# Two table-sized edits: which engine copies the inverses' PSUM products, and behind what one weight of the second feed-forward is cast

## The chip, the cores and the metric

The kernel runs on one core of a Trainium2 chip. Its time is device microseconds of one execution. The core's engines have an instruction queue each and meet only at semaphores: TensorE (PE; PEld is its weight load), VectorE (DVE), ScalarE (ACT), GpSimd (POOL), and SyncE (SP), which issues nearly all DMAs. Before the change the median of three runs was 1485.09 us (1483.22 to 1487.64).

## What is computed

One layer of a diffusion backbone: 512 latent tokens and 256 context tokens of width 1024, all in float32.

```
x   = post_ln(ALPHA*x + 0.5*gate*swiglu(modulate(x)))          # half-step feed-forward 1 (and for ctx)
p   = modulate(x) @ w_in                                        # q,k,v of both mixers, gates
o_a = neighbourhood attention over (latent grid + context)
o_b = gated delta rule, forward and backward, chunks of 64 tokens
y   = (sigmoid(ga)*(o_a @ w_pa) + sigmoid(gb)*(o_b @ w_pb)) @ w_o
x   = post_ln(ALPHA*x + gate*y)
x   = post_ln(ALPHA*x + 0.5*gate*swiglu(modulate(x)))          # half-step feed-forward 2
```

The delta rule needs, for each chunk, head and direction, the inverse of a unit lower triangular matrix:

```
m  = where(strict, (beta*k) @ k.T * decay, 0)
uw = triangular_solve(eye + m, rhs, unit_diagonal=True)
```

## The kernel before, in words

**Products.** Every large product is made in three passes: an operand is split into a rounded high part (cast on ACT, line 137, tiles `wh`, `uxh`) and the rest (subtraction on DVE, line 139, tiles `wl`, `uxl`), and PE multiplies high by high, high by low and low by high (lines 193 to 195).

**Order of the work.** The program is written as one stream of instructions; a scheduler that plays it through on a modelled timeline then sets the order on each engine. `tc.issue_after(x)` holds what stands under it back until x has been placed. So an edit of one line can reorder all engines for some distance behind it. Once set, an engine's order is fixed: an instruction that waits holds up everything behind it on its engine.

**The delta rule's stage** runs from about 785 to 957 us. The work goes over three blocks (`bi` = 0, 1, 2) of two steps (`st` = 0, 1); each step has two pairs of heads, both directions together. `grams` builds the matrices m (tiles `Bt`) and writes them to DRAM; `base_inverse` inverts their 32x32 diagonal blocks on DVE, row by row (lines 1165 and 1166, tiles `bt` and `Xt`; its matrix `L` comes from DRAM, line 1158, and its diagonal is set on POOL, line 1161), and writes the result to DRAM (line 1169). `inverse(bi, st)`, called six times, loads these blocks as `T0` and `T1` (line 1186), transposes them on DVE (1188, 1189), and joins them to 64x64 and then 128x128 inverses. It does so in a chain between PE and the engines that can read PSUM:

- PE: `py` = Bt x T0 (32x32 tiles); copy to `Y` (line 1208); PE: `p0`, `p1` from `Y`; `p0` back into `T6` (DVE, 1224), `p1` into `Tt` (ACT, 1225);
- PE: `py` = Bt x T6 (64x64 tiles); copy to `Y6` (line 1235); PE: `p1` from `Y6` and `Tt`; `p1` into `Tt` (ACT, 1243).

There is one `T6` (`NT6` = 1): the copies of `T0` into it (ACT, 1199) for the next inverse wait until PE has read it for this one. `scan_step` then uses `Tt`: `r` (DVE, 1266), a PE product with `Tt`, `vn` (DVE, 1275), `ktail` (ACT, 1280), products with both, the state `S` (DVE, 1290). Between these short products PE works off the projections' tiles (`pm`, lines 193 to 195), put there by `turn`, so that a chain's waits are covered as far as the order allows. ACT also casts these projections' weights and spills their results.

**The second feed-forward** begins at about 1121 us. The last product before it, with `w_o`, ends token block by token block: for blocks t = 0 to 3 `finish2` adds the residual, normalises twice, and makes `y` (ACT, line 130; its bias `nb` is made on DVE, line 129), which PE transposes (line 148) into `uxh`, `uxl`. The first four hidden tiles are computed on the first half of the tokens while blocks 2 and 3 are still being normalised. The weights' casts for these tiles are held by a table, `ws.behind`: for weight j a pair, behind which ACT's cast and DVE's subtraction may be placed. The eighth weight (j = 7) was held on ACT behind `y` of block 2.

Of the kernel before, what the change touches and what calls it, by code (L numbers as in the profile page):

```python
# [58 lines left out]
def body(ctx, tc, I, out, dbg=None):  # L59
    nc = tc.nc  # L60
    V, S, G, T = nc.vector, nc.scalar, nc.gpsimd, nc.tensor
# [15 lines left out]
    def tl(p, shape, tag, bufs=1, dt=F32):  # L77
        uid[0] += 1
        return p.tile(list(shape), dt, name=f"{tag}_{uid[0]}", tag=tag, bufs=bufs)
# [265 lines left out]
    def rows(w, ks):  # L345
        return [w[k * P:(k + 1) * P, :] for k in ks]
# [23 lines left out]
    def order1():  # L370
        t = lambda fs: [I["up1"][2 * f + j] for f in fs for j in range(2)]
        dn = lambda a, b: rows(I["dn1"], range(a, b))
        o = t(range(F0, N1)) + t(range(N1)) + dn(0, N1) + dn(0, N1 - 2)
        return [(w, "x") if j % 3 == 1 else w for j, w in enumerate(o)]
# [60 lines left out]
    ws = Stream(wp, order1(), WB, 1)  # L435
# [242 lines left out]
    ws = Stream(wp, o, WB, 1)  # L678
# [90 lines left out]
    ws = ws2  # L769
# [284 lines left out]
    def mm(*a, **k):  # L1054
        last[0] = T.matmul(*a, **k).ins  # L1055
# [14 lines left out]
    def turn(kind, i):  # L1070

        due[0] += RATE[kind][i]
        while due[0] >= 1:
            due[0] -= 1
            with tc.issue_after(last[0]):
                next(fills, None)
# [102 lines left out]
    def inverse(bi, st, rd, Bts):  # L1179


        T0 = tl(gq, [P, 8, 32], "T0", 2)
        T1 = tl(gq, [P, 8, 32], "T1", 2)
        for dst, d in ((T1, 0), (T0, 1)):
            for q in range(2):
                nc.sync.dma_start(dst[q:P:2, 4 * d:4 * d + 4], bass.AP(rd.tensor, rd.offset + (2 * d + q) * 16384 + st * 2048, [[32, 64], [2 * 2048, 4], [1, 32]]))
        fl = lambda t, m: t[:, m:m + 4].rearrange("p m c -> p (m c)")
        V.transpose(fl(T0, 0), fl(T1, 0))
        V.transpose(fl(T1, 4), fl(T0, 4))
        blk = [slice(32 * b, 32 * b + 32) for b in range(4)]  # L1190


        T6, Tt = T6s[inv_n[0] % NT6], Tts[inv_n[0] % NTT]
        inv_n[0] += 1
        sysm = lambda b: slice(0, 4) if b % 2 else slice(4, 8)
        bt = lambda k, b: Bts[k % 2][:, k // 2 + (0 if b else 2)]
        for b, r in enumerate(blk):
            o = 32 * (b % 2)
            S.copy(T6[r, :, o:o + 32], T0[r])
            G.tensor_copy(Tt[r, :, 32 * b:32 * b + 32], T1[r])  # L1200
        py = tl(pgq, [P, 4, 32], "pi", 2)
        for k in range(4):
            for b, r in enumerate(blk):
                q, m = blk[b ^ 1], k if b % 2 else 4 + k
                mm(py[r, k, :], bt(k, b % 2)[q, r], T0[q, m, :], start=True, stop=True, tile_position=(32 * (b ^ 1), 32 * b))
        turn("i", bi)
        Y = tl(gq, [P, 4, 32], "Y2", 2)
        V.tensor_copy(Y[:], py[:])
        p0 = tl(pgq, [P, 4, 32], "pi", 2)
        p1 = tl(pgq, [P, 4, 32], "pi", 2)  # L1210
        for k in range(4):
            for b, r in enumerate(blk):
                m = k if b % 2 else 4 + k
                mm(p0[r, k, :], T1[r, m, :], Y[r, k, :], start=True, stop=True, tile_position=(32 * b, 32 * b))
        turn("i", bi)
        for k in range(4):
            for b, r in enumerate(blk):
                m = k if b % 2 else 4 + k
                mm(p1[blk[b ^ 1], k, :], Y[r, k, :], T1[r, m, :], start=True, stop=True, tile_position=(32 * b, 32 * (b ^ 1)))
        turn("i", bi)  # L1220
        for b, r in enumerate(blk):
            o = 32 * ((b + 1) % 2)
            q = blk[b ^ 1]
            V.tensor_scalar(T6[r, sysm(b), o:o + 32], p0[r], -1.0, None, op0=ALU.mult)
            S.activation(Tt[q, sysm(b), r], p1[q], AF.Copy, scale=-1.0)

        hb = [slice(0, 64), slice(64, 128)]
        py = tl(pgq, [P, 4, 64], "pi", 2)
        for k in range(4):
            for b in range(2):  # L1230
                m = k if b else 4 + k
                mm(py[hb[b], k, :], bt(k, b)[hb[1 - b], hb[b]], T6[hb[1 - b], m, :], start=True, stop=True, tile_position=(64 * (1 - b), 64 * b))
        turn("i", bi)
        Y6 = tl(gq, [P, 4, 64], "Y6")
        V.tensor_copy(Y6[:], py[:])
        p1 = tl(pgq, [P, 4, 64], "pi", 2)
        for k in range(4):
            for b in range(2):
                m = k if b else 4 + k
                mm(p1[hb[1 - b], k, :], Y6[hb[b], k, :], Tt[hb[b], m, hb[b]], start=True, stop=True, tile_position=(64 * b, 64 * (1 - b)))  # L1240
        turn("i", bi)
        for b in range(2):
            S.activation(Tt[hb[1 - b], sysm(b), hb[b]], p1[hb[1 - b]], AF.Copy, scale=-1.0)
        return [[Tt[:, 4 * d + 2 * i + p] for d in range(2) for i in range(2)] for p in range(2)]
# [99 lines left out]
    def inv_of(bi, st):  # L1344
        inv[(bi, 2 * st)], inv[(bi, 2 * st + 1)] = inverse(bi, st, rds[bi], [res[(bi, 2 * st + p)][0] for p in range(2)])
# [278 lines left out]
    ys, norms = [], []  # L1624
# [26 lines left out]
    ws = Stream(wp, [(w, key(j)) if key(j) else w for j, w in enumerate(src)], WB, 2)  # L1651
    ws.extra = {"b": (wb, 4, wp, WB), "c": (wc, 2, wp, WB)}

    ws.behind = {j: (norms[t]["y"], norms[u][m]) for j, t, u, m in ((2, 1, 2, "nb"), (3, 1, 2, "nb"), (4, 2, 3, "x2"), (5, 2, 3, "x2"), (6, 2, 3, "nb"), (7, 2, 3, "nb"))}

    def h2(p, n):
        hs.append((tl(p, [P, NX], "hh", n, F32R), tl(p, [P, NX], "hl", n, F32R)))
# [128 lines left out]
    ws = Stream(wp, [(w, "d") if j % 6 > 1 else w for j, w in enumerate(rows(I["dn2"], range(NF)))], WB, 2)  # L1786
# [23 lines left out]
    for t in range(4):  # L1810
        h = tl(lp, [P, D], "h4", 2)
        n, m = (512, D) if t < 3 else (D // PIECES, 512)
        st = tl(lp, [P, PIECES, 6], "bst", 4)
        x2 = tl(lp, [P, D], "x2", 2)
# [123 lines left out]
```

## Time and profile before

| | before |
|---|---|
| median of the runs | 1485.09 us |
| profiled execution, its own time | 1482.26 us |
| its span, first to last instruction | 1480.5 us |
| mean granted TensorE clock | 0.995 |
| PE busy | 1430.8 us (97%) |
| DVE busy | 1144.0 us (77%) |
| ACT busy | 661.7 us (45%) |
| DMA queue of SP | 229.40 MB, 45.8% of 16 engines' span |

A matmul's end is modelled, so PE's share says that it is seldom without an instruction, not that it runs at its peak. The timeline view lists an engine's instructions with start, length and, in brackets, how long the engine stood idle before one and what released it. `T<-rd` means: into tile T from rd. The profile drops the numbers of tiles; the order listings below keep them, so that two tiles of one name can be told apart there.

### The profile page before, as it was taken

To read this page: it belongs to the slowest core of one execution; us is meant where nothing else is said; L and a number is where in the kernel's file an instruction comes from. 1 tells how busy PE (TensorE), PEld (TensorE's weight loads), DVE (VectorE), ACT (ScalarE), POOL (GpSimd) and SP (SyncE) were. 2 spreads that over 40 slices of the span, in tenths; PEclk is the share of its full clock that TensorE was granted. 3 is DMA by queue.
4 is the path that set the end of the run, shared out by engine and by line. 5 is a ranking of instruction groups with operands and counts; after the bars stand their busy time and mean duration, and the time that the engine had idled before them with its cause. 6 is when DMAs were issued, how large, how long until landed. Compare 5 with 4: busy or idle time off the path is not lost.

```text
span 1480.5 us, 23912 instructions
## 1 busy us (share of the span) xinstructions
PE 1430.8 (97%) x9117; PEld 1255.9 (85%) x9117; DVE 1144.0 (77%) x1975; ACT 661.7 (45%) x1090; POOL 214.6 (14%) x262
## 2 busy tenths in 40 slices
PE   6999999999999999999999899999999999999997
PEld 4789889999997777888877778877788999998886
DVE  8688869999987666768787885676668799886627
ACT  5435523434333387545544434376426454444310
POOL 1000000000000111223201001352321022220001
PEclk9999999999999999999999999999999999999999
DMA  9677764444569444222476523283344133234722
GB/s 377 206 250 250 240 232 172 162 161 165 164 212 400 181 160 150 79 93 94 153 227 209 163 68 126 93 302 108 120 157 171 38 129 114 94 106 144 257 99 85
DMA packets 109236, 248.56 MB, mean 168 GB/s; under 512 B 29049, under 2 KB 44481, under 8 KB 109121
## 3 DMA queue, kind: packets, MB, share of 16 engines
q1 hardware_dynamic: 104480, 229.40, 45.8%
q0 software_dynamic: 3056, 12.33, 2.2%
q10 hardware_dynamic: 1586, 5.32, 0.9%
q8 instruction: 71, 1.16, 0.3%
q14 instruction: 43, 0.35, 0.1%
HBM read 215.50 MB, written 31.50 MB: 167 GB/s over the span
## 4 chain that ended last, share of the span: by engine, by line
PE 72%; DVE 11%; DMA 8%; issue 3%; ACT 3%; POOL 2%; SPq 1%; DVEq 0%; POOLq 0%; ACTq 0%
PE ps L212 17%; PE ps L534 5%; PE ps L536 5%; PE ps L535 5%; PE pm L193 4%; PE pm L194 4%; PE pm L195 4%; PE ps L193 3%; PE ps L195 3%; PE ps L194 3%; PE ps L1712 3%; PE ps L1714 3%; PE ps L1713 3%; PE pc L1055 2%; DVE wl L139 2%
## 5 line engine op out<-in xcount | busy, mean ns | idle before, releaser
L137 ACT CAST wh<-wr 128x1024 fp32r<-128x1024 f32 (+1 forms) x184 | 185.4, 1013 | 270.6 <-PE pm L194 67.5
L139 DVE TENSOR_TENSOR wl<-wr,wh 128x1024 fp32r<-128x1024 f32 (+1 forms) x184 | 225.1, 1228 | 102.2 <-ACT wh L137 101.8
L193 PE MATMUL pm<-uxh,wh 128*128 128x512 f32 x320 | 131.3, 410 | 0.2
L195 PE MATMUL pm<-uxh,wl 128*128 128x512 f32 x320 | 126.3, 395 | 1.0 <-DVE wl L139 1.0
L194 PE MATMUL pm<-uxl,wh 128*128 128x512 f32 x320 | 126.0, 394 | 0.0
L212 PE MATMUL ps<-wh,hx 128*128 128x512 f32 x352 | 96.3, 391 | 1.1 <-ACT wh L137 1.1
L212 PEld LDWEIGHTS ps<-wh,hx 128*128 128x128 f32 x352 | 65.9, 188 | 15.7 <-ACT wh L137 1.9
L281 DVE SCALAR_TENSOR_TENSOR adap<-wr,crow 128x1024 f32<-128x1024 f32 x61 | 74.3, 1218 | 0.7 <-ACT crow L289 0.3
L195 PEld LDWEIGHTS pm<-uxh,wl 128*128 128x128 f32 x320 | 60.5, 189 | 14.2 <-DVE wl L139 1.2
L114 POOL TENSOR_TENSOR rs<-ve,mhalf 128x1 f32<-128x1 f32 (+2 forms) x46 | 50.3, 1095 | 141.5 <-DVE ve L110 139.1
L193 PEld LDWEIGHTS pm<-uxh,wh 128*128 128x128 f32 x320 | 60.7, 190 | 11.3 <-ACT u L152 0.4
L194 PEld LDWEIGHTS pm<-uxl,wh 128*128 128x128 f32 x320 | 60.7, 190 | 10.4
L193 PE MATMUL ps<-uh,wh 128*128 128x256 f32 (+1 forms) x208 | 68.2, 328 | 0.4 <-ACT wh L137 0.4
L194 PE MATMUL ps<-ul,wh 128*128 128x256 f32 (+1 forms) x208 | 67.3, 324 | 0.0
L195 PE MATMUL ps<-uh,wl 128*128 128x256 f32 (+1 forms) x208 | 67.1, 325 | 0.0
L194 PE MATMUL ps<-uxl,wh 128*128 128x256 f32 (+1 forms) x192 | 60.5, 317 | 0.8 <-DVE uxl L139 0.8
L137 ACT CAST wh<-ra 128x1024 fp32r<-128x1024 f32 x31 | 32.6, 1052 | 62.1 <-PE ps L535 20.2
L195 PE MATMUL ps<-uxh,wl 128*128 128x256 f32 (+1 forms) x192 | 60.2, 317 | 0.0
L193 PE MATMUL ps<-uxh,wh 128*128 128x256 f32 (+1 forms) x192 | 59.7, 317 | 0.0
L534 PE MATMUL ps<-ur,wh 128*128 128x384 f32 x168 | 56.5, 336 | 0.0
L535 PE MATMUL ps<-ur,wh 128*128 128x384 f32 x168 | 56.4, 336 | 0.0
L534 PE MATMUL ps<-uh,wh 128*128 128x384 f32 x168 | 56.4, 336 | 0.0
(502 smaller groups left out, 4246.8 us busy)
## 6 DMA issues: line engine op xcount, KB each, us to landing
wr<-in_w_adaT_dram SPq DMA_DIRECT2D x64, 512.0 KB, 4.6
wr<-in_up_dram SPq DMA_DIRECT2D x56, 512.0 KB, 3.4
wr<-in_win_dram SPq DMA_DIRECT2D x52, 512.0 KB, 3.4
wr<-in_dn_dram SPq DMA_DIRECT2D x51, 512.0 KB, 3.7
ra<-in_up_dram SPq DMA_DIRECT2D x24, 512.0 KB, 4.3
rb<-in_up_dram SPq DMA_DIRECT2D x18, 512.0 KB, 3.3
ra<-in_w_adaT_dram SPq DMA_DIRECT2D x16, 512.0 KB, 4.5
wr<-in_w_o_dram SPq DMA_DIRECT2D x8, 512.0 KB, 4.3
```

Source lines behind the costliest of these rows:

```text
L114: G.tensor_tensor(rs[:], ve[:], mhalf[:, 0:n], ALU.pow)
L137: marks["hi"] = S.copy(hi, src).ins
L139: marks["lo"] = V.tensor_tensor(lo, src, hi.bitcast(F32), ALU.subtract).ins
L193: T.matmul(ps, a, uh[:, k, :], start=(k == 0), stop=False)
L194: T.matmul(ps, a, ul[:, k, :], start=False, stop=False)
L195: marks["mm"] = T.matmul(ps, b, uh[:, k, :], start=False, stop=(k == nk - 1)).ins
L212: T.matmul(banks[t][d][:, c0:c1], a[:, sl], b[:, d * 512 + c0:d * 512 + c1], start=first and j == 0, stop=last and j == 2)
L281: V.scalar_tensor_tensor(pr[:], raw[:], 1.0, crow, op0=ALU.mult, op1=ALU.mult, accum_out=col[:, c:c + 1])
L534: T.matmul(ps[:], a, mh, start=k == 0, stop=False)
L535: T.matmul(ps[:], a, ml, start=False, stop=False)
L536: T.matmul(ps[:], b, mh, start=False, stop=k == 3)
L1712: T.matmul(ps[:], a, uh[:, k], start=k == 0, stop=False)
```

## The change

Two copies of inner products, from PSUM to SBUF, go from DVE to ACT in each of the six calls of `inverse`; and the eighth weight's cast on ACT is held behind `y` of the last token block (3) instead of block 2. What DVE's subtraction for that weight is held behind stays as it was.

```diff
@@ inverse
         Y = tl(gq, [P, 4, 32], "Y2", 2)
-        V.tensor_copy(Y[:], py[:])
+        S.copy(Y[:], py[:])
...
         Y6 = tl(gq, [P, 4, 64], "Y6")
-        V.tensor_copy(Y6[:], py[:])
+        S.copy(Y6[:], py[:])
@@ second feed-forward
     ws.behind = {j: (norms[t]["y"], norms[u][m]) for j, t, u, m in
-        (..., (6, 2, 3, "nb"), (7, 2, 3, "nb"))}
+        (..., (6, 2, 3, "nb"), (7, 3, 3, "nb"))}
```

The order changes from the first of these copies (about 795 us) to the end of attention (about 1045 us) on all engines, and again at the eighth weight; elsewhere it is the same. Three places matter.

**DVE, end of the second block's base inverse.** `Xt_7791` from `bt_8060` is the last row of block 1's base inverse; `bt_8317` is the first of block 2's, which needs the next `L` from DRAM; `r_8267` belongs to `scan_step` of block 1, first step, first pair, and `wl_8219` is a projection's weight.

```order
+L1166 TENSOR_REDUCE Xt_7791<-bt_8060 128x16
 L139 TENSOR_TENSOR wl_8219<-wr_8216,wh_8218 128x1024
-L1166 TENSOR_REDUCE Xt_7791<-bt_8060 128x16
+L1165 TENSOR_TENSOR bt_8317<-L_8303,Xt_8305 128x2
+L1166 TENSOR_REDUCE Xt_8305<-bt_8317 128x1
 L1266 SCALAR_TENSOR_TENSOR r_8267<-pc_8256,neg_5210,vtok_5217 128x128
 L1266 SCALAR_TENSOR_TENSOR r_8267<-pc_8256,neg_5210,vtok_5218 128x128
```

The old base inverse now ends ahead of the weight's subtraction, and the new one's first row stands ahead of `r`. Behind `r` the order is now: two more rows of the new base inverse, half of the third, and then `vn_8277`, which before stood after one of them.

**ACT and PE, the inverse of block 1, first step.** `T_1560` is its `T0`, `T_1275` the one `T6`, `Y_1563` its `Y`, `Y_1567` its `Y6`; `pi_8451` and `pi_8452` are `p0` and `p1`, `pi_8493` the second `py`, `pi_8504` the second `p1`. `T_1623` and `Y_1626` are those of the next inverse. First ACT:

```order
 L1225 ACTIVATE Tt_1276_6934<-pi_8452 32x4x32 x4
-L1199 COPY T_1275_6933<-T_1623_8755 32x8x32 x4
+L1199 COPY T_1275_6933<-T_1623_8755 32x8x32
+L1235 COPY Y_1567_8502<-pi_8493 128x256
+L1199 COPY T_1275_6933<-T_1623_8755 32x8x32 x3
 L1243 ACTIVATE Tt_1276_6934<-pi_8504 64x4x64 x2
+L1208 COPY Y_1626_8788<-pi_8771 128x128
 L137 CAST wh_8583<-wr_8581 128x1024
```

`Y6` stands between the first and the second of the four copies into `T6` for the next inverse. Then PE at the same inverse, from the product with `vn` on:

```order
-L1055 MATMUL pi_8451<-Y_1563_8449,T_1561_8417 32x32 x13
+L1055 MATMUL pi_8432<-T_1560_8416,Bt_7332 32x32
 L1055 MATMUL pc_8382<-vn_8375,ktail_8377 128x128 x4
-L1055 MATMUL pi_8451<-Y_1563_8449,T_1561_8417 32x32 x3
-L1055 MATMUL pi_8452<-T_1561_8417,Y_1563_8449 32x32 x16
 L1055 MATMUL pc_8539<-S_1529_8298,kT_5221 128x128
```

```order
+L1055 MATMUL pi_8451<-Y_1563_8449,T_1561_8417 32x32 x16
+L1055 MATMUL pi_8452<-T_1561_8417,Y_1563_8449 32x32 x16
 L1055 MATMUL pi_8493<-T_1275_6933,Bt_7249 64x64 x2
 L1055 MATMUL pi_8493<-T_1275_6933,Bt_7332 64x64 x2
```

The products with `Y` have moved behind a product with the state and six projection matmuls, to stand directly ahead of the product with `T6`.

**ACT, the last token block of the second feed-forward.** `wh_11491` is the eighth weight, `y_2135` the last block's `y`, `hh_11443` and `fs_11678` belong to the third hidden tile.

```order
 L273 ACTIVATE fs_11678<-ps_11628 128x256
+L130 ACTIVATE y_2135_11408<-xr_11389,nb_11418,rs_2139_11416 128x1024
 L137 CAST wh_11491<-wr_11489 128x1024
-L130 ACTIVATE y_2135_11408<-xr_11389,nb_11418,rs_2139_11416 128x1024
+L137 CAST hh_11443<-fs_11678 128x256
 L152 ACTIVATE u_2191_11683<-ps_11684,colx_72 128x128 x4
-L137 CAST hh_11443<-fs_11678 128x256
 L152 ACTIVATE u_2191_11683<-ps_11695,colx_72 128x128 x4
```

The cast and `y` have changed places, and the hidden tile's cast has moved ahead of the first four scalings.

More of the change, by code (lines that the diff above doesn't have):

```diff
@@ L1652, in body @@
     ws.extra = {"b": (wb, 4, wp, WB), "c": (wc, 2, wp, WB)}
-    ws.behind = {j: (norms[t]["y"], norms[u][m]) for j, t, u, m in ((2, 1, 2, "nb"), (3, 1, 2, "nb"), (4, 2, 3, "x2"), (5, 2, 3, "x2"), (6, 2, 3, "nb"), (7, 2, 3, "nb"))}
+    ws.behind = {j: (norms[t]["y"], norms[u][m]) for j, t, u, m in ((2, 1, 2, "nb"), (3, 1, 2, "nb"), (4, 2, 3, "x2"), (5, 2, 3, "x2"), (6, 2, 3, "nb"), (7, 3, 3, "nb"))}
     def h2(p, n):
```

## The prediction

> **What bounds the kernel now.** I read the page's busy shares first, then PE's timeline for its waits, then who kept the releaser.
>
> ```profile
> PE 1430.8 (97%) x9117; PEld 1255.9 (85%) x9117; DVE 1144.0 (77%) x1975; ACT 661.7 (45%) x1090; POOL 214.6 (14%) x262
> ```
>
> PE has an instruction nearly all the time, and neither edit takes one from it. So the change is worth what it does to PE's waits, and to its clock, and no more. In PE's timeline the waits in the reach of the edits are these (start, length, what, and in brackets the idle time before and its releaser):
>
> ```profile
> 794.26 0.56 PE L1055 MATMUL pi<-T,Bt 32*32 32x32 f32 x32 [3.43 <-DMA T<-rd]
> 820.32 0.68 PE L1055 MATMUL pi<-T,Bt 64*64 64x64 f32 x16 [0.86 <-DVE T L1224]
> 825.62 0.68 PE L1055 MATMUL pi<-Tt,Y 64*64 64x64 f32 x16 [2.37 <-DVE Y L1235]
> 846.86 1.13 PE L1055 MATMUL pc<-vn,ktail 128*128 128x128 f32 x8 [2.60 <-DVE bt L1165]
> 859.73 0.68 PE L1055 MATMUL pi<-T,Bt 64*64 64x64 f32 x16 [0.49 <-DVE T L1224]
> 862.01 0.68 PE L1055 MATMUL pi<-Tt,Y 64*64 64x64 f32 x16 [1.60 <-DVE Y L1235]
> 863.55 2.08 PE L1055 MATMUL pc<-r,Tt 128*128 128x128 f32 x8 [0.30 <-ACT Tt L1243]
> 892.90 1.13 PE L1055 MATMUL pc<-vn,ktail 128*128 128x128 f32 x8 [0.54 <-DVE vn L1275]
> 903.57 1.00 PE L1055 MATMUL pc<-r,Tt 128*128 128x128 f32 x6 [0.56 <-DVE r L1266]
> 1142.33 1.09 PE L148 MATMUL ps<-ident,y 128*128 128x128 f32 x8 [1.64 <-ACT y L130]
> ```
>
> Of twelve copies to `Y` or `Y6` only two are waited for, both `Y6`: 2.37 + 1.60 = 3.97 us. The 3.43 us before the first inverse end with a load and lie ahead of the edit. The waits from 820 to 904 us sum to 9.32 us; that is all the first edit can win, beside the clock. The second edit's place is the last row.
>
> The clock by short stretches (columns: stretch, its length, busy us of PE, PEld, DVE, ACT, POOL, then the granted clock, DMA share, GB/s):
>
> ```profile
> 794.00:796.00 2.00, 1.74 (x35) 1.51 (x36) 1.64 (x8) 1.61 (x4) 1.26 (x4) 0.61 0.95 302
> 824.00:826.00 2.00, 0.38 (x13) 0.41 (x15) 2.00 (x8) 1.31 (x2) 0.00 (x0) 1.00 0.00 0
> 844.00:846.00 2.00, 0.26 (x3) 0.07 (x1) 0.51 (x4) 0.00 (x0) 0.16 (x1) 1.00 0.61 232
> 864.00:866.00 2.00, 2.00 (x10) 1.90 (x10) 0.85 (x3) 0.00 (x0) 0.00 (x0) 0.50 0.00 0
> ```
>
> After the 3.43 us wait the clock drops to 0.61, and to 0.50 after the three waits around 860 us; the single waits of 2.37 and 2.60 us leave it at 1.00. At 863.55 us eight halves of a product take 2.08 us, against 1.13 us at 846.86 us. So the loss near 864 us is about 1 us there and some tenths behind it: I count 1.3 us.
>
> **The copies, part by part.** Durations come from the groups by line, 785 to 930 us (busy, mean ns of one, idle before), and from one ACT copy of the same shape elsewhere:
>
> ```profile
> L1165 DVE TENSOR_TENSOR bt<-L,Xt 128x2 f32<-128x2 f32 (+30 forms) x62 | 21.5, 346 | 3.7 <-POOL L L1161 2.5
> L139 DVE TENSOR_TENSOR wl<-wr,wh 128x1024 fp32r<-128x1024 f32 x14 | 17.0, 1216 | 0.2 <-ACT wh L137 0.2
> L1266 DVE SCALAR_TENSOR_TENSOR r<-pc,neg,vtok 128x128 f32<-128x128 f32 x32 | 9.3, 341 | 4.4 <-PE pc L1055 4.4
> L1275 DVE TENSOR_TENSOR vn<-pc,beta 128x512 f32<-128x512 f32 x10 | 6.9, 686 | 2.7 <-PE pc L1055 2.7
> L1224 DVE TENSOR_SCALAR T<-pi 32x128 f32<-32x128 f32 x24 | 6.8, 284 | 1.4 <-PE pi L1055 1.1
> L1140 DVE TENSOR_TENSOR At<-kq,Dt 128x512 f32<-128x512 f32 x4 | 2.8, 692 | 1.3 <-DMA kq<-kqd 1.3
> L1235 DVE COPY Y<-pi 128x256 f32<-128x256 f32 x6 | 2.5, 420 | 1.2 <-PE pi L1055 1.2
> L1208 DVE COPY Y<-pi 128x128 f32<-128x128 f32 x6 | 1.7, 276 | 0.0
> L1280 ACT ACTIVATE ktail<-ktok,etg 128x128 f32<-128x128 f32 x36 | 11.5, 390 | 13.4 <-PE pc L1055 13.4
> L1199 ACT COPY T<-T 32x256 f32<-32x256 f32 x24 | 9.7, 403 | 7.9 <-issue 4.4 <-DMA T<-rd 2.9 <-DVE r L1266 0.3
> L1225 ACT ACTIVATE Tt<-pi 32x128 f32<-32x128 f32 x24 | 6.4, 268 | 8.0 <-PE pi L1055 7.7
> L1243 ACT ACTIVATE Tt<-pi 64x256 f32<-64x256 f32 x12 | 4.5, 378 | 10.3 <-PE pi L1055 10.3
> L1729 ACT COPY sn<-ps x15: 352/365/373, 1173.1 to 1336.1; 128x256 f32<-128x256 f32 x15
> ```
>
> DVE loses 2.5 + 1.7 = 4.2 us; ACT gains 6 x 0.27 (row 1225, as long in the free direction) + 6 x 0.365 (row 1729) = 3.8 us. Neither sum is on the path: one copy costs the same on either engine. What counts is what stands ahead of it.
>
> *Block 0, second step (820 and 825 us).* On DVE `Y6` stood behind a backlog that began when DVE waited for a decay load:
>
> ```profile
> 808.83 0.63 SPq L1124 DMA_DIRECT2D Dt<-gcd  x1
> 814.70 1.14 DVE L1128 SCALAR_TENSOR_TENSOR Dt<-Dt,gcum,cst 128x128 f32<-128x128 f32 x4 [2.43 <-DMA Dt<-gcd]
> ```
>
> That load now goes out about 1.2 us earlier: the `Y6` ahead of its producer is gone (0.42) and a spill has left the queue ahead of it (the rest, with its wait). But four DVE steps (a product of line 1140, 0.69, and three steps of the base inverse, some 0.4 each) now stand between it and `T6`'s write (1224), so this write comes 0.8 us later than now, and PE's wait of 0.86 becomes 1.35. `Y6` on ACT stands behind an exponential, released by a DVE step after that write, and four `ktail` (4 x 0.31 by start-to-start, 0.39 each): it ends some 0.9 us after PE wants it, not 2.37. With one product moved ahead of the first wait the stretch ends about **-1.2 us** earlier. Bounds: -3.2 (both waits vanish) to +0.8 (the later write, and `Y6` as late as now).
>
> *Block 1's first scan (846 us).* Now:
>
> ```profile
> 839.57 2.09 ACT L1159 COPY L<-Ltr 64x1024 f32<-64x1024 f32 x1
> 840.07 0.42 SPq L1158 DMA_DIRECT2D L<-bd  x1
> 845.38 0.16 DVE L1165 TENSOR_TENSOR bt<-L,Xt 128x2 f32<-128x2 f32 x1 [2.24 <-POOL L L1161]
> DMA to landing us min/median/max: 2.3/2.4/5.0
> ```
>
> The last line is for the four loads of `L` at this place. The slow one, 5.0 us, was issued at 840.07, behind a spill and ahead of a weight and a result that filled the DMA engines; `vn` stood behind the row that waited for it. In the change both `L` loads go out together once the old base inverse is done (1.2 us earlier by the above, and 0.34 more, start to start, for the `Y6` that has left DVE ahead of it: 837.5 us), into idle DMA engines, so I take 2.4 us: 840.3. ACT's copy into `L` then decides, 841.66 less 1.2. So `bt` starts at 841, and `r`, now behind it, at 841.3; four `r` (1.1), the product, `vn` (0.69): the product with `vn` starts at 844.2, against 846.86, of which 1.2 was already counted: **-1.5**. Bounds: -2.6 (no wait left) to +2.0 (L as late as now, with `r` behind it).
>
> *The loads of `T0`, `T1` (847 to 855 us).* These now go out some 3 us earlier, all eight before the spill that split them:
>
> ```profile
> 846.93 3.91 SPq L1186 DMA_DIRECT2D T<-rd  x6
> 849.70 0.31 DVE L1188 STREAM_TRANSPOSE T<-T 128x128 f32<-128x128 f32 x1 [0.24 <-DMA T<-rd]
> ```
>
> The first transpose is 2.8 us behind the first issue. But DVE now has three transposes, of loads issued up to 2.6 us apart, ahead of the scan's `S` and `r`; before, one. `r` is held by the third and `vn` by a weight's subtraction (1.22) that moved ahead of it: two new waits of about 1.2 and 0.9, of which 0.8 is earlier arrival. **+1.3**; bounds 0 to +2.5.
>
> *Block 1, first step (860 us).* The products with `Y` now stand directly ahead of the product with `T6`. Between them lie four writes of line 1224 (1.2): wait 1.1 where 0.49 was. Then `Y6`, behind one copy into `T6` that itself waits for that product (0.40 + 0.365 and two hops: 1.0 where 1.60 was). Then `Tt`, behind three copies (1.2) and 0.77 of its own: 1.0 where 0.30 was. 3.1 against 2.39, less half a us of covered small products: **+0.2**. The clock drops here as now. Bounds: -3.7 (the 2.39 and 1.3 of clock) to +1.0.
>
> [...]
>
> *Behind it.* `vn` at 892.90 now precedes the weight's subtraction (1.22): **-0.5** (0 to -0.54). In block 2 the copies leave DVE early enough, `r` at 903.57 stays behind a subtraction and two transposes, and before the last inverse `r` and `T6`'s write follow each other closely: **+0.1** (-0.6 to +1.4). In attention the order changes without a step added or taken: **0** (-1.5 to +1.5).
>
> **The weight's cast.** From ACT's and DVE's timelines:
>
> ```profile
> 1139.47 0.21 DVE L129 TENSOR_SCALAR nb<-bmv,rs 128x1 f32<-128x1 f32 x1
> 1140.09 1.05 ACT L137 CAST wh<-wr 128x1024 fp32r<-128x1024 f32 x1 [0.66 <-DMA wr<-in_up_dram]
> 1141.04 1.24 ACT L130 ACTIVATE y<-xr,nb,rs 128x1024 f32<-128x1024 f32 x1
> ```
>
> `y` could start at 1139.7 when `nb` is made, and waits for a weight's load and cast instead. It now starts 1.4 us earlier, so PE's 1.64 becomes 0.2. The cast ends at 1141.9 and its subtraction at 1143.1; PE needs them behind the transposes and the 24 products of another weight, after 1144. **-1.4** (0 to -1.64).
>
> **Sum**, in order: -1.2 - 1.5 + 1.3 + 0.2 - 0.5 + 0.1 + 0 - 1.4 = -3.0 us. From the profiled execution's 1482.26 us that is 1479.3. The runs' median lies 2.8 us above that execution; from 1485.09 the same sum gives **1482.1 us**.
>
> **Rivals.**
>
> *The waits go altogether.* ACT is half idle, so `Y6` may find it free: 2.37 + 1.60 + 0.30 vanish, with the waits that short the clock stays up (1.3), and `L`, `vn` and the cast give their 1.5, 0.5 and 1.4: 9.0 us, 1476.1. For it: ACT is 45% busy. Against it: the order puts `Y6` behind steps that wait for the same chain.
>
> *`r` behind the next `L`.* If `L` lands at 845.2 as now, `r` starts at 845.7 and the product with `vn` at about 848.6, 1.7 later than now; PE's two waits there then approach 5 us, and the clock drops as after the 3.43 (1.5). With the transposes' 1.3, 0.2, 0.4 in block 2, -0.5 and -1.4: +3.2, 1488.3. It decides from `L` landing after about 844. For it: 5.0 us is what one of these loads took. Against: the weight that shared its time now goes out behind it.
>
> *The edits only move waits.* The first edit's terms cancel and the cast's gain is met by a later wait (the next at 1176 us stands behind DVE steps): 1485.
>
> **How the numbers follow.** Forecast 0.50 (own range 1479.5 to 1485), waits gone 0.25, only moved 0.12, `r` behind `L` 0.13. About 0.3%, 4.5 us, is what a measurement of this kernel can tell from none: faster means under 1480.6, slower over 1489.5. Faster: nearly all of the first rival and a quarter of the forecast, 0.36; slower: under half of the case with `r` behind `L`, 0.06; same 0.58. The range leaves out the ends of both outer cases: 1475.5 to 1488.3.
>
> **What would show it.** PE's product with `Y6` in block 0 waits about 0.9 us and comes after a wait of over 1 us for `T6`; the product with `vn` near 844 waits about 1.1, with `L`'s loads at 2.4 us; the transposes near 848 wait for loads; three waits near 1 us and a dropped clock at block 1's first step; `y` follows `nb` at once, and PE's wait there is under 0.5. I am wrong on the first edit if `L` lands later than 844, or if the clock stays at 1.00 near 864 us; on the second if `y` starts late for another reason.

## The result, and the profile after

The changed kernel takes 1480.4 us (median; 1475.12 to 1484.23) where the kernel before takes 1483.95 us (1479.68 to 1487.64) beside it: a ratio of 0.9977, with a 95% interval of 0.9968 to 0.9985. That is 3.5 us less, against a forecast of 3.0 us. The predicted 1482.1 us started from the first median of 1485.09 us.

The profiled executions alone would mislead. The one of the changed kernel is its slowest, 1484.23 us, 2 us above the one before (1482.26 us). So the difference of the two spans says nothing here, and the places have to be compared one by one. The page's busy shares of the changed kernel:

```profile
PE 1436.5 (97%) x9117; PEld 1261.7 (85%) x9117; DVE 1143.8 (77%) x1963; ACT 665.7 (45%) x1102; POOL 214.5 (14%) x262
```

ACT has 4.0 us more, as the copies' durations gave (3.8): between 785 and 930 us its twelve copies to `Y6` and `Y` took 373 and 262 ns each, where DVE's took 420 and 276. DVE has 0.2 less where 4.2 was expected. Its twelve copies are gone, but other steps took longer: above all the four subtractions for `obl` in attention (line 139, 1055 ns each where they took 707) and those of the 128x512 weights (997 where 945), together 2.3 us. Why they are slower is not shown. The waits say more. PE's timeline, changed kernel, the rows that answer to those of before:

```profile
795.74 0.93 PE L1055 MATMUL pi<-T,Bt 32*32 32x32 f32 x32 [3.14 <-DMA T<-rd]
825.51 0.68 PE L1055 MATMUL pi<-Tt,Y 64*64 64x64 f32 x16 [0.41 <-issue]
843.49 1.26 PE L1055 MATMUL pc<-r,Tt 128*128 128x128 f32 x8 [0.29 <-DVE r L1266]
845.82 1.13 PE L1055 MATMUL pc<-vn,ktail 128*128 128x128 f32 x8 [1.07 <-DVE Xt L1166]
859.27 0.68 PE L1055 MATMUL pi<-T,Bt 64*64 64x64 f32 x16 [1.21 <-DVE T L1224]
860.89 0.68 PE L1055 MATMUL pi<-Tt,Y 64*64 64x64 f32 x16 [0.94 <-ACT Y L1235]
862.84 1.73 PE L1055 MATMUL pc<-r,Tt 128*128 128x128 f32 x8 [0.88 <-ACT Tt L1243]
924.96 1.26 PE L1055 MATMUL pc<-r,Tt 128*128 128x128 f32 x8 [0.44 <-DVE r L1266]
970.21 0.66 PE L1482 MATMUL po<-pT,vw 128*64 128x128 f32 x8 [1.82 <-DVE vw L1438]
1141.26 1.09 PE L148 MATMUL ps<-ident,y 128*128 128x128 f32 x8 [0.75 <-ACT y L130]
```

The same products can be laid side by side, since their starts cut the time into pieces. The changed kernel starts its first inverse 1.48 us later than the kernel before (795.74 against 794.26 us), because of waits and a drop of the clock near 743 us, ahead of the edit (a wait of 2.08 us for a weight's subtraction, and a clock of 0.50 from 744 to 746 us). From there on:

| from, to | forecast | this pair of profiles | how it comes out |
|---|---|---|---|
| first inverse to block 0's product with `Y6` | -1.2 | 31.36 to 29.77: -1.6 | waits of 0.86 and 2.37 became 0 and 0.41 (-2.8); more clock lost (+1.7) |
| to the product with `vn` | -1.5 | 21.24 to 20.31: -0.9 | 2.60 became 0.29 and 1.07 |
| to the product behind block 1's first step | +1.3 + 0.2 | 16.69 to 17.02: +0.3 | 0.49, 1.60, 0.30 became 1.21, 0.94, 0.88 |
| to the second product with `oacc` | -0.5 + 0.1 | 94.38 to 93.92: -0.5 | 0.54 and 0.56 became 0.44 |
| attention, to the last product with `pT` that PE waits for | 0 | 84.77 to 86.84: +2.1 | a new wait of 1.82 for `vw`; PE's idle time in all 1.11 to 3.34 |
| to the last block's `y` in the second feed-forward | -1.4 | 99.63 to 97.66: -2.0 | -1.3 of it in the last 20 us, where 1.64 became 0.75; the rest in an unchanged place (a wait of 0.61 at 1103 us is gone) |
| sum | -3.0 | -2.6 | |

In the first row the clock hides a part of the gain. Behind the first inverse the granted clock of the kernel before is 0.61 and 0.53 in the 2 us stretches from 794 us, then 1.00; in this execution of the changed kernel it is 0.75, 0.50, 0.50 and 0.55. Stretch length times what is missing to 1.00 is 1.7 us lost against 3.4 us. The wait before it, 3.14 us for a load, lies ahead of the edit.

At the last of these products the changed kernel has turned 1.48 us late into 1.07 us early. Behind it, in code that is the same, it loses 3.0 us (the last section says how).

### The profile page after: what moved, and what is told of

Its sections match the earlier page's. It is cut to its first block, busy times and chain, and to the rows that moved or that the text cites. A ratio compares the mean times of both kernels' runs of the same rounds, so it can differ in the third digit from the quotient of the medians.

```text
span 1482.4 us, 23911 instructions
## 1 busy us (share of the span) xinstructions
PE 1436.5 (97%) x9117; PEld 1261.7 (85%) x9117; DVE 1143.8 (77%) x1963; ACT 665.7 (45%) x1102; POOL 214.5 (14%) x262
## 4 chain that ended last, share of the span: by engine, by line
PE 71%; DVE 12%; DMA 8%; issue 3%; ACT 3%; POOL 2%; SPq 1%; DVEq 0%; ACTq 0%; POOLq 0%
PE ps L212 15%; PE ps L534 4%; PE ps L535 4%; PE ps L536 4%; PE pm L193 4%; PE pm L194 4%; PE pm L195 4%; PE ps L193 4%; PE ps L194 4%; PE ps L195 4%; PE ps L1713 3%; PE ps L1712 3%; PE ps L1714 3%; PE pc L1055 2%; DVE wl L139 2%
## 5 line engine op out<-in xcount | busy, mean ns | idle before, releaser
L137 ACT CAST wh<-ra 128x1024 fp32r<-128x1024 f32 x31 | 32.6, 1052 | 62.8 <-PE ps L535 20.2
```

The source lines that it names most:

```text
L137: marks["hi"] = S.copy(hi, src).ins
```

## What the experiments showed

Each kernel stands beside runs of the kernel before on its own chip; its diff is against the kernel that its expectation names.

### The copies alone

```diff
-        V.tensor_copy(Y[:], py[:])
+        S.copy(Y[:], py[:])
...
-        V.tensor_copy(Y6[:], py[:])
+        S.copy(Y6[:], py[:])
```

> The two copies on ACT in all six inverses, the eighth weight's cast as before. The order of the delta rule's stage and of attention is that of the changed kernel; a few rows of the late convolution stage stand elsewhere. The two profiles give, place by place: the second step of block 0 -1.6, the product with vn -0.9, block 1 up to r +0.3, block 2 -0.4, attention +2.1 (PE waits 1.82 us for vw, line 1438). Theory A, the wait for vw comes from the new order: the copies alone are worth -0.6 us (ratio 0.9996) and the wait of 1.5 to 2 us for vw is here again. Theory B, the wait for vw was an accident of that execution (a late load): no such wait here, and the copies alone are worth -2.6 us (ratio 0.9982). Rival: the copies only move waits, ratio 1.000 with as much PE wait between 795 and 905 us as before (12.7 us).

Measured: 1480.81 against 1484.77 us, ratio 0.9981 (0.9969 to 0.9993). Its PE timeline in attention:

```profile
966.15 0.66 PE L1482 MATMUL po<-pT,vw 128*64 128x128 f32 x8 [1.59 <-DVE vw L1438]
```

The wait for `vw` is here again, so theory B's reason falls: it is no accident of one execution. Yet the ratio is what theory B gave (0.9982), and theory A's 0.9996 lies outside the interval: the sum over places that it used, from one pair of profiles, priced the copies too low. The rival that waits are only moved is out, since the interval ends below 1.

### The weight's cast alone

```diff
-        (..., (6, 2, 3, "nb"), (7, 2, 3, "nb"))}
+        (..., (6, 2, 3, "nb"), (7, 3, 3, "nb"))}
```

> Only the eighth weight's cast held behind y of token block 3. Forecast term: -1.4 us (ratio 0.9991), PE's wait near 1142 us for y from 1.64 to under 0.9, and attention as before (wait for vw under 0.5 us). Rival, the gain is met by a later wait: ratio 1.000, and the wait near 1176 us grows by what the one at 1142 us loses.

Measured: 1481.82 against 1484.77 us, ratio 0.9982 (0.9970 to 0.9995). Its PE timeline:

```profile
969.20 0.66 PE L1482 MATMUL po<-pT,vw 128*64 128x128 f32 x8 [0.24 <-DVE vw L1438]
1141.18 1.09 PE L148 MATMUL ps<-ident,y 128*128 128x128 f32 x8 [0.53 <-ACT y L130]
1175.02 0.39 PE L1714 MATMUL ps<-t14h,sl 128*128 128x256 f32 x1 [1.19 <-DVE sl L139]
```

The wait for `y` falls to 0.53 us and the one near 1176 us stays at its 1.19: no later wait takes the gain. The expected 0.9991 lies inside the interval, a ratio of 1.000 does not. The two parts alone sum to 5.5 us (0.19% and 0.18%) where both together give 3.5; with intervals of nearly 2 us on each, that is no contradiction, and no proof that they add.

### Y2 alone and Y6 alone

```diff
 # the first run has this edit alone:
-        V.tensor_copy(Y[:], py[:])
+        S.copy(Y[:], py[:])
 # the second run has this one alone:
-        V.tensor_copy(Y6[:], py[:])
+        S.copy(Y6[:], py[:])
```

> Only the copies to Y2 on ACT, Y6 on DVE, the cast as before. In the first two blocks PE's order is nearly that of before, in attention that of the changed kernel. Theory A (the new order in attention costs 2 us): ratio 1.0005 to 1.0015, Y6 waited for 2.4 and 1.6 us as before, and 1.5 to 2 us of wait for vw. Theory B (accident): ratio 0.9995 to 1.0003, no wait for vw over 0.5 us.

> Only the copies to Y6 on ACT, Y2 on DVE, the cast as before. PE's order is that of the changed kernel but for a few rows of the late stage. If the gain of the copies is Y6's alone, as the forecast has it (no copy to Y2 is waited for), this is worth what both copies are: ratio within 0.0007 of the run with both. Rival, Y2 on DVE in this order is waited for: waits with Y as their releaser and 0.3 us or more on DVE, ratio 0.001 worse than the run with both copies.

Measured: `Y2` alone 1486.12 against 1484.77 us, ratio 1.0016 (1.0004 to 1.0028), slower; `Y6` alone 1482.21 us, 0.9990 (0.9976 to 1.0004). PE's timeline, first with `Y2` alone, then with `Y6` alone:

```profile
824.37 0.68 PE L1055 MATMUL pi<-Tt,Y 64*64 64x64 f32 x16 [2.37 <-DVE Y L1235]
...
859.78 0.41 PE L1055 MATMUL pi<-Tt,Y 64*64 64x64 f32 x7 [1.60 <-DVE Y L1235]
...
970.81 0.66 PE L1482 MATMUL po<-pT,vw 128*64 128x128 f32 x8 [1.58 <-DVE vw L1438]
```

```profile
810.65 0.55 PE L1055 MATMUL pi<-Y,T 32*32 32x32 f32 x32 [0.87 <-DVE Y L1208]
897.90 0.46 PE L1055 MATMUL pi<-Y,T 32*32 32x32 f32 x22 [0.49 <-DVE Y L1208]
```

With `Y2` alone both waits for `Y6` stand to the hundredth as before, attention takes the new order with its wait, and the kernel loses. So the gain of the two copies hangs on `Y6`, but `Y6` alone does not show it (1 lies inside its interval), and `Y2` is no bystander: in the order that `Y6` on ACT brings, `Y2` left on DVE is waited for, 0.87 and 0.49 us, which the rival had. The forecast's sentence that no copy to `Y` is waited for held only for the old order.

### The wait for vw taken away

```diff
...
-            for _ in fills:
-                pass
+            for j in range(len(FILLS) * FS - done[0], 0, -1):
+                with tc.issue_after(marks["vwt"]) if j == 1 else nullcontext(): next(fills)
```

(`marks["vwt"]` is the last transpose that `vw` is copied from.)

> The changed kernel, with the last part of the last projection (six matmuls and its spill) held on PE behind the transposes that vw is copied from, as these matmuls stood by themselves before the change. In the four profiles with the new order of attention (the changed kernel, both copies, Y2 alone, Y6 alone) PE waits 1.58 to 1.82 us for vw; in the two with the old one 0 and 0.24. Theory: this wait is the price that the moved copies pay in attention, by order alone. Then the wait goes under 0.5 us and the kernel is 1.3 to 1.8 us faster than the changed one: ratio to before 0.9965 to 0.9968 where the changed kernel has 0.9977. Rival: PE has as much to do in attention whatever the order, and the wait goes elsewhere (other waits for vw or pT between 965 and 1045 us grow by over 1 us): ratio 0.9977.

Measured: 1482.4 against 1484.1 us, ratio 0.9986 (0.9976 to 0.9997). The product that waited for `vw` now starts without a wait:

```profile
968.83 0.66 PE L1482 MATMUL po<-pT,vw 128*64 128x128 f32 x8
```

Attention lasts 86.72 us (956.74 to 1043.46), as long as with the wait (86.84). The theory's ratio of 0.9965 to 0.9968 lies outside the interval, the rival's 0.9977 inside. But the edit did more than take the wait away. These are the stretches of attention in the kernel before, the changed kernel and this one (columns: stretch, its length, busy us of PE and number of its matmuls, then the other engines, granted clock, DMA share, GB/s):

```profile
957.93:1042.70 84.77, 83.66 (x717) 65.15 (x717) 61.21 (x91) 59.59 (x136) 33.38 (x39) 1.00 0.57 198
956.76:1043.60 86.84, 83.50 (x717) 65.23 (x717) 63.27 (x91) 59.72 (x136) 32.01 (x39) 1.00 0.57 193
956.74:1043.46 86.72, 84.47 (x717) 65.04 (x717) 60.78 (x91) 59.78 (x136) 33.56 (x39) 1.00 0.58 193
```

The same 717 matmuls keep PE busy for 83.66 and 83.50 us in the first two, and idle for 1.11 and 3.34 us. So the 2.1 us by which attention grew is idle time, most of it the wait for `vw`. In this run PE idles 2.25 us, 1.1 less, and is busy for 84.47 us, 1.0 more: the hold also set PE's order anew, and between 979 and 983 us single score products (`sc`) now stand among the projection matmuls. That this new order is what the 1.0 us went to is not shown. So the run does not show that the wait was without a price; it shows that this edit costs about as much in attention as it gains.

In the other profiles PE is busy here for 83.4 to 83.8 us, and the length goes with the idle time. In the old order it lasts 84.77, 85.62 and 85.15 us (before, the cast alone, the hold on the old kernel below), with 1.1 to 1.9 us idle; with both copies on ACT and the new order 86.39 to 86.84 us, with 2.9 to 3.3 us idle; with `Y2` or `Y6` alone 87.39 and 86.59 us, with 4.0 and 3.1. In the next run, which has the old order almost unchanged, it lasts 86.80 us with 3.04 us idle, though PE waits only 0.37 us for `vw` there: two waits for `pT`, 1.12 and 0.90 us, make up most of it. Why these grow is not settled.

### More cover in block 1's inverses

```diff
-    RATE = {..., "i": (1.5, 0, 0), ...}
+    RATE = {..., "i": (1.5, 0.2, 0), ...}
```

> The changed kernel, with projection matmuls put between the products of block 1's inverses (0.2 of a projection's part for each product, where it was 0): two times six matmuls, 1.4 us each, now stand inside the first step's chain, and the attention stage comes out in the order of before. Theory: PE's wait of 1.21 us for T6's write is covered, so PE idles under 2 us in that chain and the clock does not fall there: 1.2 + 1.7 us, and without the wait for vw 1.6 us more: up to 4.5 us under the changed kernel, ratio 0.9947. If the clock falls all the same: 2.8 us, ratio 0.9958. Rival: the matmuls are only taken from another place where they covered a wait (block 2, 880 to 957 us): waits there grow by 1 us or more, ratio 0.9968 to 0.9977.

Measured: 1480.47 against 1484.1 us, ratio 0.9972 (0.9959 to 0.9985). Its PE timeline:

```profile
862.02 0.72 PE L1055 MATMUL pi<-Tt,Y 64*64 64x64 f32 x16 [1.83 <-ACT Y L1235]
863.96 2.08 PE L1055 MATMUL pc<-r,Tt 128*128 128x128 f32 x8 [0.64 <-ACT Tt L1243]
1000.33 0.43 PE L1482 MATMUL po<-pT,vw 128*64 128x128 f32 x2 [1.12 <-ACT pT L1471]
```

The wait of 1.21 us for `T6`'s write is covered as meant, and most of it comes back one step further on: `Y6` is waited for 1.83 us where it was 0.94. The clock falls there in this run as well (0.50 from 863.96 to 867.96 us). So the time is the rival's, but not for its reason: the wait came back inside the chain, and not in block 2, where PE's waits between 880 and 957 us (0.24, 0.45 and 0.40 us against one of 0.44, and in both kernels 1.15 us before the second product with `oacc`) grew by 0.65 us, less than the 1 us that it named. Matmuls put into one gap of a chain covered that gap and lengthened the next.

### The copies into T6 behind the chain

```diff
-            S.copy(T6[r, :, o:o + 32], T0[r])
+            with tc.issue_after(marks["Tt6"]) if "Tt6" in marks else nullcontext():
+                S.copy(T6[r, :, o:o + 32], T0[r])
...
```

(`marks["Tt6"]` is the last ACT copy into `Tt` of the inverse before, line 1243.)

> The changed kernel, with the four copies into T6 for the next inverse (line 1199) held on ACT behind the last copy into Tt of this one (line 1243), so that the Y6 copy has none of them ahead of it. In the changed kernel PE waits at block 1's first step 1.21 (T6's write), 0.94 (Y6) and 0.88 us (Tt), and the clock falls to half for 3.4 us behind them, which costs 1.7 us. If the forecast's step holds (Y6 behind one copy, Tt behind three), the Y6 wait falls by 0.4 and the Tt wait to near 0, about 1 us, ratio 0.9970; if with the shorter chain the clock stays up as well, 2.7 us, ratio 0.9959. Rival: T6's next write then comes later and the waits return in the next inverse (lines 1224 and 1235, 880 to 930 us): ratio 0.9977 or more.

Measured: 1479.02 against 1484.1 us, ratio 0.9967 (0.9954 to 0.9979). The interval holds the ratios of the theory and of its rival, so the time does not decide between them; the timelines do. First what ACT did in the changed kernel, then PE's timeline and the stretches (with the granted clock ahead of the last two columns) of the kernel with the hold:

```profile
859.95 0.40 ACT L1199 COPY T<-T 32x256 f32<-32x256 f32 x1 [0.71 <-PE pi L1055]
860.38 0.37 ACT L1235 COPY Y<-pi 128x256 f32<-128x256 f32 x1
860.77 1.23 ACT L1199 COPY T<-T 32x256 f32<-32x256 f32 x3
862.02 0.77 ACT L1243 ACTIVATE Tt<-pi 64x256 f32<-64x256 f32 x2
```

```profile
856.78 0.68 PE L1055 MATMUL pi<-Tt,Y 64*64 64x64 f32 x16 [0.52 <-issue]
858.32 1.16 PE L1055 MATMUL pc<-r,Tt 128*128 128x128 f32 x8 [0.47 <-ACT Tt L1243]
```

```profile
858.00:860.00 2.00, 1.69 (x12) 1.56 (x12) 1.86 (x6) 1.94 (x6) 0.00 (x0) 1.00 0.00 0
860.00:862.00 2.00, 2.00 (x36) 1.55 (x35) 1.86 (x6) 1.42 (x3) 0.00 (x0) 1.00 0.00 0
```

`Y6` stood 0.43 us behind the first copy (859.95 to 860.38) and `Tt` 1.2 us behind the other three, as the forecast had read from the order. With them gone the waits are 0.52 and 0.47, and the clock stays at 1.00. The wait of 1.21 us for `T6`'s write is gone too, but for another reason: the hold changed PE's order along, and the products with `Y` stand earlier again, as in the kernel before. So of the 2.0 us by which the waits fell (3.03 to 0.99), 1.2 goes with PE's order and 0.8 with the copies, and which of the two keeps the clock up is not shown. The waits that the rival put into the next inverse are not there: PE's timeline has none of 0.2 us or more between 859 and 950 us. The changed kernel in the same place:

```profile
862.00:864.00 2.00, 1.16 (x7) 1.16 (x8) 1.82 (x5) 0.91 (x4) 0.00 (x0) 0.81 0.03 8
864.00:866.00 2.00, 2.00 (x7) 1.69 (x7) 1.36 (x3) 0.00 (x0) 0.00 (x0) 0.50 0.00 0
866.00:868.00 2.00, 2.00 (x34) 1.39 (x33) 1.58 (x5) 1.26 (x2) 0.00 (x0) 0.83 0.00 0
```

### The same hold on the old kernel, and both kernels again

> The kernel before, with the same hold on the copies into T6 as in the run before this one and nothing else: only ACT's order differs, at three places. Y and Y6 are on DVE. If the gain of that run belongs to the hold alone, this is as much faster than the kernel before as that one was than the changed kernel: about 0.1%, ratio 0.9990, and the clock stays up near 860 us. If it needs Y6 on ACT, only the wait for Tt can go here (0.30 to 0.47 us), PE still idles about 2.2 us for T6's write and Y6 there, the clock falls for 3.4 us as before, and the ratio is 0.9995 to 1.0003.

> The changed kernel again, beside the next run on the same chip. If the ledger of waits is right (delta rule's stage and attention -2.1, cast -1.1) the ratio is 0.9978 as at first. In its profile: waits near 1.2, 0.9 and 0.3 to 0.9 us at block 1's first step, half clock for 3.4 us (1.7 us lost) or twice as long (3.4 us) behind them, and a wait of 1.5 to 1.9 us for vw.

> The changed kernel with the copies into T6 held behind the last copy into Tt, again. Theory: with under 1.5 us idle in block 1's first step the clock stays at 1.00 from 835 to 872 us, in this profile as in the first, and the kernel is 1.5 to 2.7 us faster than the changed one of the same chip (ratio to before 0.9967 against 0.9978). [...]

On the kernel before, the hold shows no gain: 1485.92 against 1485.97 us, ratio 0.9996 (0.9983 to 1.0010). Its waits near 860 us for `Y6` and `Tt` are still there (1.60 and 0.30 in the kernel before), and the clock falls behind them (0.50 from 861.26 to 863.26 us):

```profile
859.72 0.47 PE L1055 MATMUL pi<-Tt,Y 64*64 64x64 f32 x9 [1.60 <-DVE Y L1235]
861.26 2.08 PE L1055 MATMUL pc<-r,Tt 128*128 128x128 f32 x8 [0.48 <-ACT Tt L1243]
```

So what the hold does near 860 us needs `Y6` on ACT. On the same chip the changed kernel came to 1481.59 us, ratio 0.9958 (0.9941 to 0.9975), and the one with the hold to 1479.67 us, 0.9951 (0.9936 to 0.9965). The expected 0.9978 lies just outside the changed kernel's interval. One kernel thus gave 0.9977 and 0.9958 on two occasions, so a difference of 0.001 or 0.002 between ratios that were not measured beside each other says little. The changed kernel's repeat, PE's timeline and the stretches that follow:

```profile
860.16 1.12 PE L1055 MATMUL pi<-Tt,Y 64*64 64x64 f32 x16 [0.94 <-ACT Y L1235]
862.14 2.08 PE L1055 MATMUL pc<-r,Tt 128*128 128x128 f32 x8 [0.28 <-ACT Tt L1243]
969.74 0.66 PE L1482 MATMUL po<-pT,vw 128*64 128x128 f32 x8 [1.51 <-DVE vw L1438]
```

```profile
860.00:862.00 2.00, 1.70 (x48) 1.48 (x48) 1.79 (x7) 1.90 (x7) 0.00 (x0) 0.51 0.03 8
862.00:864.00 2.00, 1.86 (x9) 1.86 (x9) 1.16 (x3) 0.24 (x2) 0.00 (x0) 0.50 0.00 0
864.00:866.00 2.00, 2.00 (x7) 1.61 (x6) 1.67 (x4) 0.00 (x0) 0.00 (x0) 0.50 0.00 0
866.00:868.00 2.00, 2.00 (x35) 1.31 (x34) 1.62 (x4) 1.54 (x2) 0.00 (x0) 0.78 0.00 0
```

The hold's repeat has the same two waits, 0.52 and 0.47 us, and behind them:

```profile
858.00:860.00 2.00, 1.52 (x42) 1.41 (x42) 1.80 (x6) 1.89 (x6) 0.00 (x0) 1.00 0.04 8
```

The clock near 860 us stayed at 1.00 in both profiles with the hold on the changed kernel, and fell to 0.50 in all ten others. Its loss there is each stretch's length times what is missing to 1.00, summed: 1.7 us in the first profile of the changed kernel (0.38 + 1.00 + 0.34), 3.4 us in this one (0.98 + 1.00 + 1.00 + 0.44). So the theory of the hold stands. Two profiles do not exclude that the clock stayed up by chance: the last section has a wait of 2.37 or 2.38 us behind which it fell in one of four executions. In time it is less clear: on the chip they share, the medians put the hold 1.9 us under the changed kernel, and the two pairs of ratios (0.9967 and 0.9977, 0.9951 and 0.9958) 1.0 to 1.5 us, with intervals that overlap. In the profiles the stretch from the product with `vn` to the second product with `oacc` takes 106.8 and 107.1 us with the hold and 110.9 and 111.5 us in the changed kernel, so this stage is shorter in both. That the whole is faster than the changed kernel is likely and not shown; that it is faster than the kernel before is shown.

## Why the prediction was right, and where it was not

**The direction, the size and the range** held: 3.5 us measured, 3.0 forecast, under the 0.3% that was set as the bound of "same". What carried the sum was the reading of the order against the durations, place by place. But two of its terms were wrong, +1.3 that came to about 0 and 0 that came to +1.4 us or more, and that they nearly cancel is luck. A third, `L`'s, was too large. Nor do the profiles add up to the whole: from the first inverse to the last block's `y`, the two without either edit take 348.1 and 348.9 us and the changed kernel's two 345.5 and 347.4, which is 2.0 us less in the mean, where the runs say 3.5 (2.2 to 4.7 by the interval).

**Block 0** came out in size, and in mechanism only in part. `Y6` on ACT stands behind the four `ktail`, as read; the profile gives PE's idle time ahead of the product with `Y6` no releaser ("issue"), but the product starts 0.1 us behind the copy's end (825.41 and 825.51 us). PE waits 0.41 us there in this profile and 0.85 to 0.98 us in the seven others with `Y6` on ACT (forecast 0.9). The wait for `T6`'s write was forecast to grow from 0.86 to 1.35. In this profile it is gone, which the forecast had only as its bound, and the longer stretch of half clock took up to 1.7 us of that gain back. In the changed kernel's repeat, where the clock lost 1.7 us here as in the kernel before, the waits are 0.82 and 0.98 us and the stretch takes 30.27 us, 1.1 less than before: close to the forecast of 1.2.

**The loads of `L`** went as read, but the term is smaller than forecast. The forecast let the first row of the new base inverse start at 841 and the product with `vn` at 844.2 us. Changed kernel, DVE's timeline:

```profile
842.83 0.16 DVE L1165 TENSOR_TENSOR bt<-L,Xt 128x2 f32<-128x2 f32 x1 [1.77 <-POOL L L1161]
847.01 0.31 DVE L1188 STREAM_TRANSPOSE T<-T 128x128 f32<-128x128 f32 x1 [1.27 <-DMA T<-rd]
```

Less the 1.48 us by which this execution was late from the start, the row stands at 841.35 and the product (845.82) at 844.34 us. The slowest of the four loads took 2.9 us, not 5.0. The rival "`r` behind the next `L`" was ruled out by this; it needed a landing after 844 us. But the 5.0 us that the forecast took as the price of the old order was the longest of four: in the other profiles with the old order here (the cast alone, `Y2` alone, the hold on the old kernel) PE's wait for the product with `vn` was 0.88, 1.82 and 1.68 us instead of 2.60. The stretch from the product with `Y6` takes 20.3 to 21.2 us in these four and 20.2 to 20.5 us in the eight with `Y6` on ACT, so the term is worth nearer 0.5 than 1.5 us.

**The loads of `T0`, `T1`: the first wrong term.** The forecast made PE pay +1.3 us for transposes that wait for loads. DVE does wait, 1.27 us in the second row above. But PE shows no wait between 845.82 and 859.27 us: it had projection matmuls for all of it. The term was a DVE wait put down as PE's without asking what PE had left to do; it measures about 0.

**Block 1's first step** was forecast at waits of 1.1, 1.0 and 1.0 us and has 1.21, 0.94 and 0.88, and the clock drop is there. The drop was priced at 1.3 us; in the two profiles it costs 1.7 and 3.4 us of granted clock. That a shorter chain could keep the clock up was in the first rival only; the two profiles with the hold show it (waits of 0.52 and 0.47 us, clock at 1.00).

**Attention: the second wrong term.** "The order changes without a step added or taken: 0" took equal work for equal time. It measures +2.1 us in this pair and +1.4 us in the mean over the profiles, near the end of the bounds given (1.5). In all seven profiles with the new order and without the edit against it PE waits 1.5 to 1.8 us for `vw`, because a weight's subtraction moved ahead of its copies on DVE and the projection matmuls that had covered them were already spent. PE's busy time stays the same and its idle time grows by 2.2 us, so the step that failed is the one from equal work to equal waits. What the wait alone is worth is open: the run that took it away also gave PE an order in which it was busy for 1.0 us more.

**The cast** was worth its term. `y` now waits for its bias `nb` alone, and the cast stands behind it; changed kernel, ACT's timeline:

```profile
1139.96 1.24 ACT L130 ACTIVATE y<-xr,nb,rs 128x1024 f32<-128x1024 f32 x1 [0.29 <-DVE nb L129]
1141.11 1.03 ACT L137 CAST wh<-wr 128x1024 fp32r<-128x1024 f32 x1
```

In this pair PE's wait fell from 1.64 to 0.75 us, not to the 0.2 of the forecast. Over the profiles the wait for the last `y` is 1.0 to 2.0 us in five kernels without the edit and 0.3 to 0.8 us in seven with it, about 1.2 us against a forecast of 1.4.

**The rivals.** The waits did not go altogether (3.03 us stand in block 1's first step alone); that they are only moved is excluded by the interval.

## What to carry to other kernels

When a copy moves to an engine that is half idle, read what will stand ahead of it there: the half-idle ACT still made `Y6` wait for the next inverse's copies, and when those were moved away PE's waits there fell from 3.03 to 0.99 us (0.8 of it by the copies) and the clock stayed at 1.00, which is likely worth 1 to 2 us more. A wait on an engine that is not the bottleneck becomes a term of the sum only after it is asked what the bottleneck engine still has to do at that moment. And an edit that takes a wait away is judged by the whole stage: the wait of 1.8 us for `vw` vanished in one run, but PE's busy time grew by 1.0 us with the new order, and the stage stayed as long as it was (86.72 us, where it was 86.84).

## What the runs showed of the hardware

**The losses of clock came in two sizes.** In stretches of 2 us or less, from the first inverse to 1168 us, each loss of granted clock that lies whole in them sums to 1.70 to 1.72 us or to 3.40 to 3.42 us, in all twelve profiles; the lowest clock in them is 0.50, at which that is 3.4 or 6.8 us of time. Which of the two it is changes from run to run at the same place: behind waits of 1.21 and 0.94 us the changed kernel lost 1.7 us near 864 us, and behind 1.14 and 0.94 us 3.4 us in the other profile, as shown above. Whether the clock falls at all changes too. Before block 0's product with `Y6` PE waits 2.37 or 2.38 us in four profiles, and the clock stayed at 1.00 in three of them (the kernel before, `Y2` alone, the hold on the old kernel); in the fourth, the cast alone, it fell:

```profile
824.38 0.68 PE L1055 MATMUL pi<-Tt,Y 64*64 64x64 f32 x16 [2.38 <-DVE Y L1235]
```

```profile
826.00:828.00 2.00, 2.00 (x6) 1.60 (x5) 2.00 (x4) 0.00 (x0) 0.00 (x0) 0.50 0.89 296
```

The clock also fell at single waits that were shorter than the 2.37 and 2.60 us of the forecast's rows. In the hold on the old kernel:

```profile
1141.25 1.97 PE L148 MATMUL ps<-ident,y 128*128 128x128 f32 x8 [2.04 <-ACT y L130]
```

```profile
1142.00:1144.00 2.00, 2.00 (x11) 2.00 (x10) 0.00 (x0) 1.60 (x5) 0.00 (x0) 0.50 0.83 215
```

With a wait of 2.04 us the clock fell to 0.50 here, where waits of 2.37 and 2.60 us in the kernel before left it at 1.00. Near 742 us the changed kernel waits 2.08 us, with 0.50 behind it, and products of 128x512 start 0.43 us apart there, 0.23 us apart once the clock is back. In the first run with the hold they start 0.43 us apart behind a wait of 1.92 us, and in the changed kernel's repeat 0.23 us apart behind one of 2.01 us. So single waits of 1.92, 2.04, 2.08 and 2.38 us came ahead of a fall, and single waits of 2.01, 2.37 and 2.60 us did not: it is not the length of the wait alone. What else decides it is not shown.

**PE ran at two paces at a granted clock of 1.00.** In the convolution stage of the second feed-forward, the same products in both kernels, with 18 steps between the first and the last row of each pair; kernel before, then changed kernel:

```profile
1272.27 0.28 PE L1712 MATMUL ps<-uxh,wh 128*128 128x256 f32 x1
...
1274.31 0.28 PE L1712 MATMUL ps<-uxh,wh 128*128 128x256 f32 x1
```

```profile
1272.69 0.28 PE L1712 MATMUL ps<-uxh,wh 128*128 128x256 f32 x1
...
1274.81 0.28 PE L1712 MATMUL ps<-uxh,wh 128*128 128x256 f32 x1
```

2.04 us and 2.12 us for 18 steps: 113 and 118 ns each, 4% apart. PE shows no wait in either piece, and the granted clock is 1.00 in both kernels from 1180 to 1340 us. In the profile of the kernel before the step is 118 ns until about 1230 us, 113 ns from there to about 1320 us, and 118 ns again; in the changed kernel's it is 118 ns all the way to 1340 us. Between 1180 and 1200 us it is 113 ns in five of the twelve profiles and 118 ns in seven. The pace is where the 3.0 us went that the changed kernel's profile lost behind 1176 us: that profile is still 1.08 us ahead at 1231 us and 1.95 us behind at 1328 us. That this and the losses of clock (1.7 or 3.4 us each) are why executions of one kernel lie up to 9 us apart (1475.12 to 1484.23 us) is an estimate. What sets the pace is not shown.
